# Turning the second layer's attention weights by VectorE squares and SBUF transfers, in place of TensorE

## The chip, the cores and the metric

The kernel runs on one core of a Trainium2 chip. The core has five engines that each run their own list of instructions in order and wait for one another by semaphores: TensorE (PE; its weight loads are shown as PEld), VectorE (DVE), ScalarE (ACT), GpSimd (POOL) and SyncE (SP), which here issues nearly all transfers. The metric is the device time of one execution in microseconds. Before the change it is 584.42 us, the median of three runs (584.39 to 584.82).

## The reference

One inference step of a two-layer decoder, for a prompt of 256 positions and 8 single sample positions, 264 columns in all, with model width 1024. The change touches the second layer's attention of the prompt, eight heads of width 64:

```python
def stick_breaking_attention(q, k, v, q_pos):
    # A[t,s] = sigmoid(z_ts) * prod_{s<j<t} (1 - sigmoid(z_tj)), strictly causal
    ...
        z = jnp.einsum('bqhd,bkhd->bhqk', qh, k).astype(jnp.float32) * scale
        before = kpos[None, :] < pos[:, None]
        log_keep = jnp.where(before, jax.nn.log_sigmoid(-z), 0.0)
        later = lax.cumsum(log_keep, axis=3, reverse=True) - log_keep
        w = jnp.where(before, jnp.exp(jax.nn.log_sigmoid(z) + later), 0.0)
        return jnp.einsum('bhqk,bkhd->bqhd', w.astype(v.dtype), v)
```

The rest of the step (the projections, the first layer, pooling, the feed-forward parts, the output norm) is not changed.

## The kernel before, in words

All weights are streamed from HBM in a fixed order, as blocks of 128×128. A tile of work is eight blocks; a transfer (`raw`) brings sixteen blocks, and three `raw` buffers take turns. ScalarE copies each tile to a high part (`wh`, L318), VectorE takes the rest as a low part (`wl`, L325), and TensorE does three matmuls of 264 columns per block (`mm`). The phases are the input projection, attention, output projection and feed-forward of each layer. The order on TensorE is written out: `run` goes through the blocks, and hooks put other work behind a block of a given number. In the second layer the order is kept as written for TensorE and for the transfers on SP (`late`); on VectorE and ScalarE a scheduler places the instructions when the program is built, and it then stays as it is.

The second layer's input projection gives u, q, k and v in this order, 32 blocks each, four tiles of 128 rows; a row tile is a pair of heads. An evicted tile of v is `v4b` (L1252). For the attention:

- `z_qk` (blocks 83 and 103) makes the scores Z of a pair in PSUM. For each head there are three squares of 128×128: queries 0 to 127 with keys 0 to 127, queries 128 to 255 with keys 0 to 127, queries 128 to 255 with keys 128 to 255. The second query block with its own keys is the third square.
- `stick` has ScalarE make sigmoids, VectorE a scan along the keys (`keep`, L1140) and a product (`w`, L1141). The product w has the queries on its partitions, 128 rows of 384 columns.
- `z_tr` turns the three squares of each head of a pair by TensorE (`pt`, three transposes of a head in one PSUM bank), and ScalarE copies a head's bank to SBUF (`pT`, L1171). The four pairs stand behind blocks 93, 102 and 122 of the input projection and block 2 of the output projection.
- `v_pair` transposes a tile of v4b (`vtp_v`), behind blocks 113, 123, 127 and block 3 of the output projection.
- `z_av` (block 8 of the output projection, right behind the sample's value matmuls `pv_l`) multiplies values with turned weights into `pav`, pair after pair.

There are four PSUM banks for `mm` and its kin and four (`at`) for Z, pt, pav and the like. Five buffers hold w, two hold keep. SP's list is one queue in order: an issue whose wait is not over holds up all issues behind it.

Of the kernel before, what the change touches and what calls it, by code (L numbers as in the profile page):

```python
# [13 lines left out]
AF = mybir.ActivationFunctionType  # L14
# [4 lines left out]
P = 128  # L19
D = 1024  # L20
KD = D // P
SEQ = 256
# [5 lines left out]
HD = 64  # L28
# [179 lines left out]
def tile_decoder_step(ctx: ExitStack, tc: tile.TileContext, a):  # L208
    nc = tc.nc
    v, s, g = nc.vector, nc.scalar, nc.gpsimd  # L210
# [14 lines left out]
    pe = TensorE()  # L225
# [13 lines left out]
    def f4(name, shape=(P, 4, T), dt=F32):  # L239
        return up.tile(list(shape), dt, tag="u", name=name)  # L240

    def mv(name):
        return [f4(f"{name}_{x}", (P, 4, TP), F32R)[:, :, X0:X0 + T] for x in "hl"]
# [4 lines left out]
    def at(name):  # L248
        return psa.tile([P, 512], F32, tag="at", name=name)
# [17 lines left out]
    def cst(n):  # L267
        o, w = _CST[n]
        return CST[:, o:o + w]
# [11 lines left out]
    def late(dst, src):  # L281
        tc.keep_in_program_order(nc.sync.dma_start(dst, src))
# [21 lines left out]
    turned = {}  # L304
# [86 lines left out]
    first, o = [], 0  # L391
# [29 lines left out]
    ident = cst("ident")  # L421
# [15 lines left out]
    class Norm:  # L437

        def __init__(self, name):
            self.name, self.acc = name, None  # L440
# [38 lines left out]
    def halves(h, l, src):  # L479
        s.activation(h, src, AF.Copy)  # L480
        v.tensor_tensor(l, src, h.bitcast(F32), ALU.subtract)  # L481
# [72 lines left out]
    def v_pair(vt, src, t, name, bank=None):  # L554
        p = (bank or at)(f"vtp_{name}{t}")
        for kb in range(2):
            pe.transpose(p[:, kb * P:(kb + 1) * P], src[:, kb * P:(kb + 1) * P], ident)
        s.activation(vt[:, :, t * P:(t + 1) * P], p[:, :2 * P].rearrange("p (b d) -> p b d", b=2), AF.Copy)

    def av(pav, vt, w, h):  # L560
        o = pav[64 * (h % 2):64 * (h % 2) + 64, :SEQ]
        pe.matmul(o, vt[:, 0, h * HD:(h + 1) * HD], w[:, :SEQ], start=True, stop=False)
        pe.matmul(o[:, P:], vt[:, 1, h * HD:(h + 1) * HD], w[:, SEQ:], start=False, stop=True)

    def gelu_set():
        tc.keep_in_program_order(s.preload_act_table_set("gelu_apprx_tanh_and_others"))
# [4 lines left out]
    def lnexp():  # L571
        tc.keep_in_program_order(s.preload_act_table_set("natural_log_exp_and_others"))
# [285 lines left out]
    vt = f4("vt0", (P, 2, 512))  # L858
# [36 lines left out]
    def s_av(t):  # L895
        if t == 0:
            catA.extend(mv("catA0"))
        w = st0.pop(("pT", t))
        pav = at(f"pav0_{t}")
        for hh in range(2):  # L900
            av(pav, vt, w[:, hh, :], 2 * t + hh)
        halves(catA[0][:, t, :SEQ], catA[1][:, t, :SEQ], pav[:, :SEQ])


# [124 lines left out]
    blk = lambda b, f, *x: hk.at(b / 8 - 1, f, *x)  # L1029
# [52 lines left out]
    for t in range(4):  # L1082
        blk(8, s_av, t)
# [24 lines left out]
    vt = f4("vt1", (P, 2, 512))  # L1108
# [6 lines left out]
    st1 = {}  # L1115
# [17 lines left out]
    def stick(w, z, t):  # L1133


        n, keep = 384, keeps[t % 2]
        for a0, a1 in ((1, P), (P + 1, n)):
            s.activation(keep[:, a0:a1], z[:, a0:a1], AF.Sigmoid, scale=-1.0)
        s.activation(w, z, AF.Sigmoid)
        v.tensor_tensor_scan(keep[:, 1:n][:, ::-1], keep[:, 1:n][:, ::-1], edge[:, 1:][:, ::-1], 0.0, ALU.mult, ALU.max)  # L1140
        v.tensor_tensor(w, w, keep[:, 1:], ALU.mult)  # L1141

    def stick_all(w, z):
# [5 lines left out]
        v.tensor_tensor_scan(keep[:, ::-1], keep[:, ::-1], edge[:, P:P + 1].to_broadcast([P, n]), 1.0, ALU.mult, ALU.max)  # L1149
        v.tensor_tensor(w[:, :n - 1], w[:, :n - 1], keep[:, 1:], ALU.mult)  # L1150

    def z_qk(t):
        pss = [at(f"Z1_{2 * t + i}") for i in range(2)]
        hd = [(q4[b:b + 64, t, :], k4[b:b + 64, t, :]) for b in (0, 64)]
        for ps, (qh, kh) in zip(pss, hd):
            pe.matmul(ps[:, 0:P], qh[:, 0:P], kh[:, 0:P], start=True, stop=False, skip_group_check=True)
        for ps, (qh, kh) in zip(pss, hd):
            pe.matmul(ps[:, P:384], qh[:, P:SEQ], kh[:, 0:SEQ], start=False, stop=True, skip_group_check=True)
        for i, ps in enumerate(pss):
            w = st1["w", 2 * t + i] = pp.tile([P, 384], F32, tag="p", name=f"w1_{2 * t + i}")  # L1160
            stick(w, ps[:, :384], 2 * t + i)
        if t == 3:
            lnexp()

    def z_tr(t):
        pT = st1["pT", t] = f4(f"pT1_{t}", (P, 2, 384))
        for hh in range(2):
            w, pt = st1.pop(("w", 2 * t + hh)), at(f"pt1_{2 * t + hh}")
            for i in range(3):
                pe.transpose(pt[:, i * P:(i + 1) * P], w[:, i * P:(i + 1) * P], ident)  # L1170
            s.activation(pT[:, hh, :], pt[:, :384], AF.Copy)  # L1171

    def z_av(t):
        if t == 0:
            catA.extend(mv("catA1"))
        pav, pT = at(f"pav1_{t}"), st1.pop(("pT", t))
        for hh in range(2):
            av(pav, vt, pT[:, hh, :], 2 * t + hh)
        halves(catA[0][:, t, :SEQ], catA[1][:, t, :SEQ], pav[:, :SEQ])

    def zs_score():
# [74 lines left out]
    blk = lambda b, f, *x: hk.at(b / 8 - 1, f, *x)  # L1256
# [5 lines left out]
    for t in range(4):  # L1262
        blk((83, 103)[t // 2], z_qk, t)
    blk(82, zs_tr)
    for t, b in enumerate((93, 102, 122, 130)):
        if b < 128:
            blk(b, z_tr, t)
    blk(84, late, a["poolp"], plp)
    blk(84, late, a["pools"], PALL)
    blk(112, late, a["k1"], k4)  # L1270
# [5 lines left out]
        blk(b, lambda t=t: v_pair(vt, v4[:, t, :], t, "v1", mmb))  # L1276
    run(orders["in1"], pick(xg), in1_evac, hk)
    hk = Hooks()
    for t, b in enumerate((93, 102, 122, 130)):
        if b >= 128:  # L1280
            blk(b - 128, z_tr, t)
    blk(3, lambda: v_pair(vt, v4[:, 3, :], 3, "v1"))
    for i in range(2):
        blk(8, sample_av_of(st1, PZ, vtiles, i, "l1"))
    for t in range(4):
        blk(8, z_av, t)
# [79 lines left out]
```

## Time and profile before

| | us |
|---|---|
| median of 3 runs | 584.42 |
| the profiled execution | 584.75 |
| its span | 583.0 |
| TensorE busy in the span | 578.1 |
| VectorE busy | 420.4 |
| ScalarE busy | 345.6 |
| second layer's attention, from Z to the last pav | 332.5 to 365.7 |

The span is the time between the first and last instruction that the profiler saw; 1.75 us lie around it. In the page's groups, a row names the line, the engine, the operation, output and inputs, the count, then busy time and the mean of one. The busy time of matmuls overlaps, since they are pipelined: a matmul of 264 columns is busy for some 0.28 us, and the next starts 0.12 us after it. In the chain, the lengths are what each piece adds to the end. In a timeline, a row gives the start, the length, the engine, the line, the operation, and in brackets the engine's idle time before it with what ended it. Line L220 is the helper of all matmuls, L223 that of all transposes on TensorE, L282 that of the transfers, so tiles tell the rows apart.

### The profile page before, as it was taken

The page shows a single profiled execution, that of the slowest core. Times are in us where ns is not written, and L with a number is a line of the kernel's source. Part 1 is how long each engine was busy: PE and PEld are TensorE (multiplying, and loading weights), DVE is VectorE, ACT ScalarE, POOL GpSimd, SP SyncE. Part 2 cuts the span into 40 slices and gives each one's busy share as a digit, 9 for nine tenths or more (in the row PEclk, how much of TensorE's full clock was granted, in tenths as well). Part 3 has the DMA queues.
Part 4 walks back from the last instruction along what each step waited for, and adds up shares of the span by engine and source line. Part 5 has one row for each costly group of instructions (what it writes and reads, how often), then busy time and mean ns, then how long its engine had stood idle before and what let it go on. Part 6 is the DMA issues. An engine that isn't in the chain of part 4 may idle for free.

```text
span 583.0 us, 12326 instructions
## 1 busy us (share of the span) xinstructions
PE 578.1 (99%) x4913; PEld 563.9 (97%) x4913; DVE 420.4 (72%) x742; ACT 345.6 (59%) x617; POOL 110.7 (19%) x107
## 2 busy tenths in 40 slices
PE   9999999999999999999999999999999999999997
PEld 8998979999999999999999897999999999999996
DVE  6999766877777777665659685587777777765441
ACT  7748955775555656654454576667646565565442
POOL 1110021222323232210120000132232222221010
PEclk9999999999999999999999999999999999999999
DMA  8997973555454545796567855254545455556501
GB/s 343 361 376 256 402 266 105 186 175 187 161 201 152 209 150 212 265 388 221 182 230 262 311 207 181 83 209 146 201 161 191 171 183 180 175 194 223 211 2 75
DMA packets 27707, 122.40 MB, mean 210 GB/s; under 512 B 3330, under 2 KB 4226, under 8 KB 16258
## 3 DMA queue, kind: packets, MB, share of 16 engines
q1 hardware_dynamic: 27648, 121.62, 58.1%
q8 instruction: 38, 0.62, 0.4%
q14 instruction: 19, 0.16, 0.1%
q10 hardware_dynamic: 2, 0.00, 0.0%
HBM read 117.65 MB, written 3.96 MB: 209 GB/s over the span
## 4 chain that ended last, share of the span: by engine, by line
PE 95%; issue 2%; DMA 1%; ACT 1%; DVE 0%; POOL 0%; POOLq 0%; ACTq 0%
PE mm L220 88%; DMA V<-in_vp 1%; PE pv_l L220 1%; PE sc L220 1%; PE pav L220 1%; PE pt L223 1%; PE warm L220 1%; PE Z L220 1%; PE S L220 1%; ACT wh L318 0%; PE pf L220 0%; DVE bv L995 0%; PE vtp_v L223 0%; PE pm L220 0%; ACT bu L1025 0%
## 5 line engine op out<-in xcount | busy, mean ns | idle before, releaser
L325 DVE TENSOR_TENSOR wl<-raw,wh 128x1024 fp32r<-128x1024 f32 x178 | 218.4, 1231 | 64.2 <-ACT wh L318 63.8
L318 ACT ACTIVATE wh<-raw 128x1024 fp32r<-128x1024 f32 x178 | 186.2, 1051 | 81.0 <-PE mm L220 70.0
L220 PE MATMUL mm<-xg_f_h,wh 128*128 128x264 f32 x704 | 197.8, 281 | 0.0
L220 PE MATMUL mm<-xg_f_h,wl 128*128 128x264 f32 x704 | 197.8, 281 | 0.0
L220 PE MATMUL mm<-xg_f_l,wh 128*128 128x264 f32 x704 | 197.5, 280 | 0.0
L220 PEld LDWEIGHTS mm<-xg_f_h,wh 128*128 128x128 f32 x704 | 131.9, 187 | 0.0
L220 PEld LDWEIGHTS mm<-xg_f_h,wl 128*128 128x128 f32 x704 | 131.9, 187 | 0.0
L220 PEld LDWEIGHTS mm<-xg_f_l,wh 128*128 128x128 f32 x704 | 131.9, 187 | 0.0
L623 POOL TENSOR_TENSOR wk<-wk 128x264 f32<-128x264 f32 x44 | 67.3, 1531 | 193.1 <-DVE wk L622 142.8
L220 PE MATMUL mm<-a_h,wl 128*128 128x264 f32 x330 | 92.7, 281 | 0.0
L220 PE MATMUL mm<-a_h,wh 128*128 128x264 f32 x330 | 92.7, 281 | 0.0
L220 PE MATMUL mm<-a_l,wh 128*128 128x264 f32 x330 | 92.6, 280 | 0.0
L480 ACT ACTIVATE a_h<-wk 128x264 fp32r<-128x264 f32 x44 | 18.6, 424 | 75.0 <-POOL wk L623 75.0
L220 PEld LDWEIGHTS mm<-a_l,wh 128*128 128x128 f32 x330 | 61.8, 187 | 0.0
L220 PEld LDWEIGHTS mm<-a_h,wl 128*128 128x128 f32 x330 | 61.8, 187 | 0.0
L220 PEld LDWEIGHTS mm<-a_h,wh 128*128 128x128 f32 x330 | 61.8, 187 | 0.0
L481 DVE TENSOR_TENSOR a_l<-wk,a_h 128x264 fp32r<-128x264 f32 x44 | 19.2, 437 | 43.2 <-ACT a_h L480 43.2
L220 PE MATMUL mm<-xg_h,wl 128*128 128x264 f32 x160 | 42.9, 290 | 0.0
L220 PE MATMUL mm<-xg_h,wh 128*128 128x264 f32 x160 | 42.7, 289 | 0.0
L220 PE MATMUL mm<-xg_l,wh 128*128 128x264 f32 x160 | 41.9, 283 | 0.0
L220 PE MATMUL mm<-xg_n_h,wl 128*128 128x264 f32 x128 | 36.9, 288 | 0.0
L220 PE MATMUL mm<-xg_n_h,wh 128*128 128x264 f32 x128 | 36.0, 281 | 0.0
(273 smaller groups left out, 934.0 us busy)
## 6 DMA issues: line engine op xcount, KB each, us to landing
raw<-in_w SPq DMA_DIRECT2D x89, 1024.0 KB, 4.8
K<-in_kt SPq DMA_DIRECT2D x32, 256.0 KB, 7.3
V<-in_vp SPq DMA_DIRECT2D x32, 256.0 KB, 6.2
raw<-in_w SPq DMA_DIRECT2D x3, 512.0 KB, 6.1
xw<-in_xw SPq DMA_DIRECT2D x3, 388.0 KB, 4.8
X<-in_x SPq DMA_DIRECT2D x4, 264.0 KB, 7.0
out_y<-y SPq DMA_DIRECT2D x3, 256.0 KB, 2.2
out_k<-k SPq DMA_DIRECT2D x1, 528.0 KB, 7.8
```

The source lines that it names most:

```text
L220: return self.keep(nc.tensor.matmul(*x, **k))
L223: return self.keep(nc.tensor.transpose(*x, **k))
L318: i = s.activation(h, src, AF.Copy)
L325: i = v.tensor_tensor(l, src, h.bitcast(F32), ALU.subtract)
L480: s.activation(h, src, AF.Copy)
L481: v.tensor_tensor(l, src, h.bitcast(F32), ALU.subtract)
L623: g.tensor_tensor(A, A, C, ALU.mult)
```

## The change

Of each head's three squares the first two, those with keys 0 to 127, are no longer turned by TensorE. When two pairs of heads are done, VectorE turns w's first 256 columns of each of these four heads in squares of 32×32 (`squares`, STREAM_TRANSPOSE), into the tile `turnN_squares`. There each square is turned, but it still lies in the 32 partitions that it came from. Transfers inside SBUF (`move`) then take the squares to the partitions of their keys, in the tile `turnN_turned`: for each of four partition groups of the source and each of four groups of the goal one transfer, which carries two times 128 columns on 32 partitions. That makes 16 transfer instructions for four heads and 32 for eight; each carries two blocks, 64 in all. They stand on SP behind the hooks of blocks 103 and 119.

The third square stays with TensorE: `z_own` turns those of four heads into one PSUM bank, behind block 102 and behind block 2 of the output projection, and one ScalarE copy of 512 columns brings them to SBUF. `av` reads the turned tile for keys 0 to 127 (columns in runs of 32) and that copy for the rest.

```diff
-    def av(pav, vt, w, h):
+    def av(pav, vt, w0, w1, h):
         o = pav[64 * (h % 2):64 * (h % 2) + 64, :SEQ]
-        pe.matmul(o, vt[:, 0, h * HD:(h + 1) * HD], w[:, :SEQ], start=True, stop=False)
-        pe.matmul(o[:, P:], vt[:, 1, h * HD:(h + 1) * HD], w[:, SEQ:], start=False, stop=True)
+        pe.matmul(o, vt[:, 0, h * HD:(h + 1) * HD], w0, start=True, stop=False)
+        pe.matmul(o[:, P:], vt[:, 1, h * HD:(h + 1) * HD], w1, start=False, stop=True)
+
+    class Turn:
+        def __init__(self, name):
+            self.name = name
+            self.src, self.dst = [f4(f"{name}_{x}", (P, 8, 4, 32)) for x in ("squares", "turned")]
+        def squares(self, i, w):
+            v.transpose(self.src[:, :, i, :], w[:, :SEQ].rearrange("p (c b) -> p c b", b=32))
+        def move(self, i):
+            for j in range(4):
+                late(self.dst[32 * j:32 * j + 32, i::4], self.src[32 * i:32 * i + 32, j::4])
+        def of(self, i):
+            return self.dst[:, :, i, :]
...
     def z_qk(t):
...
+        if t % 2:
+            turns.append(Turn(f"turn{t // 2}"))
+            for i in range(4):
+                turns[-1].squares(i, st1["w", 2 * t - 2 + i])
...
-    def z_tr(t):
-        pT = st1["pT", t] = f4(f"pT1_{t}", (P, 2, 384))
-        for hh in range(2):
-            w, pt = st1.pop(("w", 2 * t + hh)), at(f"pt1_{2 * t + hh}")
-            for i in range(3):
-                pe.transpose(pt[:, i * P:(i + 1) * P], w[:, i * P:(i + 1) * P], ident)
-            s.activation(pT[:, hh, :], pt[:, :384], AF.Copy)
+    def z_own(f):
+        pt = at(f"pt1_{f}")
+        for i in range(4):
+            pe.transpose(pt[:, i * P:(i + 1) * P], st1["w", 4 * f + i][:, SEQ:384], ident)
+        pT = st1["pT", f] = f4(f"pT1_{f}", (P, 4, P))
+        s.activation(pT, pt.rearrange("p (i q) -> p i q", q=P), AF.Copy)
...
-    for t, b in enumerate((93, 102, 122, 130)):
-        if b < 128:
-            blk(b, z_tr, t)
+    blk(102, z_own, 0)
+    for f, b in enumerate((103, 119)):
+        for i in range(4):
+            blk(b, lambda f=f, i=i: turns[f].move(i))
...
-    for t, b in enumerate((93, 102, 122, 130)):
-        if b >= 128:
-            blk(b - 128, z_tr, t)
+    blk(2, z_own, 1)
```

On VectorE the change adds eight instructions, and the scheduler places them between the others. At the end of the input projection, VectorE's list before has these rows (`w1_6` is the product of head 6, `mm856` and `mm864` are the second and third tile of v in PSUM):

```order
L1141 TENSOR_TENSOR w1_6_4743<-w1_6_4743,keep0_4105 128x384
L325 TENSOR_TENSOR wl110_4763<-raw58_4492,wh110_4762 128x8x128
L1140 SCALAR_TENSOR_TENSOR keep1_4106<-keep1_4106,edge_4103 128x383
L1252 TENSOR_TENSOR v4b_4095<-mm856_4766,R_n1_4177 128x264
L1141 TENSOR_TENSOR w1_7_4749<-w1_7_4749,keep1_4106 128x384
L325 TENSOR_TENSOR wl111_4794<-raw58_4492,wh111_4793 128x8x128
L1252 TENSOR_TENSOR v4b_4095<-mm864_4797,R_n1_4177 128x264
```

And now, at the same place:

```order
L572 STREAM_TRANSPOSE turn1_squares_4746<-w1_5_4722 128x8x32
L325 TENSOR_TENSOR wl110_4776<-raw58_4492,wh110_4775 128x8x128
L1157 TENSOR_TENSOR w1_6_4734<-w1_6_4734,keep0_4105 128x384
L1156 SCALAR_TENSOR_TENSOR keep1_4106<-keep1_4106,edge_4103 128x383
L1274 TENSOR_TENSOR v4b_4095<-mm856_4779,R_n1_4177 128x264
L572 STREAM_TRANSPOSE turn1_squares_4746<-w1_6_4734 128x8x32
L1157 TENSOR_TENSOR w1_7_4740<-w1_7_4740,keep1_4106 128x384
L325 TENSOR_TENSOR wl111_4807<-raw58_4492,wh111_4806 128x8x128
L572 STREAM_TRANSPOSE turn1_squares_4746<-w1_7_4740 128x8x32
L1274 TENSOR_TENSOR v4b_4095<-mm864_4810,R_n1_4177 128x264
```

The turns of heads 5, 6 and 7 stand ahead of the third tile of v, the last one right before it, and the split `wl110` has moved ahead of the product of head 6. In the same way a turn stands between scan and product of heads 1 and 2, and four turns stand ahead of head 4's scan.

On SP, the list before around the same place (`raw60` to `raw62` are weights, `out_k1` and `out_v1` outputs):

```order
L282 DMA V1_14_4673<-in_vp1 128x512
L282 DMA raw60_4760<-in_w 128x2048
L282 DMA out_k1<-k4b_4094 128x1056
L282 DMA raw61_4827<-in_w 128x2048
L282 DMA raw62_4977<-in_w 128x2048
L282 DMA out_v1<-v4b_4095 128x1056
```

And now:

```order
L282 DMA V1_14_4668<-in_vp1 128x512
L282 DMA turn0_turned_4604<-turn0_squares_4603 32x2x128 x16
L282 DMA raw60_4773<-in_w 128x2048
L282 DMA out_k1<-k4b_4094 128x1056
L282 DMA turn1_turned_4747<-turn1_squares_4746 32x2x128 x16
L282 DMA raw61_4856<-in_w 128x2048
L282 DMA raw62_4991<-in_w 128x2048
L282 DMA out_v1<-v4b_4095 128x1056
```

The two groups of 16 transfers stand ahead of the weight transfers raw60 and raw61, and all behind them in the queue waits until they are issued.

More of the change, by code (lines that the diff above doesn't have):

```diff
@@ L900, in s_av @@
         for hh in range(2):
-            av(pav, vt, w[:, hh, :], 2 * t + hh)
+            av(pav, vt, w[:, hh, :SEQ], w[:, hh, SEQ:], 2 * t + hh)
         halves(catA[0][:, t, :SEQ], catA[1][:, t, :SEQ], pav[:, :SEQ])
@@ L1150, in stick_all @@
         v.tensor_tensor(w[:, :n - 1], w[:, :n - 1], keep[:, 1:], ALU.mult)
+    turns = []
     def z_qk(t):
@@ L1175, in z_av @@
             catA.extend(mv("catA1"))
-        pav, pT = at(f"pav1_{t}"), st1.pop(("pT", t))
+        pav = at(f"pav1_{t}")
         for hh in range(2):
-            av(pav, vt, pT[:, hh, :], 2 * t + hh)
+            i = 2 * t % 4 + hh
+            av(pav, vt, turns[t // 2].of(i), st1["pT", t // 2][:, i, :], 2 * t + hh)
         halves(catA[0][:, t, :SEQ], catA[1][:, t, :SEQ], pav[:, :SEQ])
```

## The prediction

> **What bounds the kernel now.** I read first the page's busy shares and its chain of waits (the work that ended last, followed back from the end).
>
> ```profile
> span 583.0 us, 12326 instructions
> PE 578.1 (99%) x4913; PEld 563.9 (97%) x4913; DVE 420.4 (72%) x742; ACT 345.6 (59%) x617; POOL 110.7 (19%) x107
> PE 95%; issue 2%; DMA 1%; ACT 1%; DVE 0%; POOL 0%; POOLq 0%; ACTq 0%
> ```
>
> TensorE sets the time: 95% of the chain, with nothing between its matmuls in most stages. So what leaves TensorE is a gain, unless TensorE then waits for what does the work instead. The same chain in order of time shows what TensorE does at the places of the change (start, length, count):
>
> ```profile
> 337.85 0.66 PE pt L223 x6
> 342.48 0.66 PE pt L223 x6
> 352.25 0.66 PE pt L223 x6
> 356.23 0.66 PE pt L223 x6
> 362.85 2.80 PE pav L220 x32
> 367.29 0.44 PE po_l L223 x4
> ```
>
> The 24 transposes of the second layer's weights take 4 × 0.66 us and TensorE is on the chain at each. VectorE's 72% over the span says little here, so its timeline in this stretch comes next (start, length, engine, line; in brackets the idle time before a row):
>
> ```profile
> 336.60 0.56 DVE L1141 TENSOR_TENSOR w<-w,keep 128x384 f32<-128x384 f32 x1
> 340.92 0.55 DVE L1141 TENSOR_TENSOR w<-w,keep 128x384 f32<-128x384 f32 x1
> 343.27 0.48 DVE L1243 SCALAR_TENSOR_TENSOR catB_l<-pm,VEC,catB_h 128x264 fp32r<-128x264 f32 x1
> 344.97 0.95 DVE L1140 TENSOR_TENSOR_SCAN keep<-keep,edge 128x383 f32<-128x383 f32 x1 [1.22 <-ACT keep L1138]
> 346.03 0.56 DVE L1141 TENSOR_TENSOR w<-w,keep 128x384 f32<-128x384 f32 x1
> 346.50 0.95 DVE L1140 TENSOR_TENSOR_SCAN keep<-keep,edge 128x383 f32<-128x383 f32 x1
> 347.37 0.40 DVE L1252 TENSOR_TENSOR v4b<-mm,R_n 128x264 f32<-128x264 f32 x1
> 351.69 0.40 DVE L1252 TENSOR_TENSOR v4b<-mm,R_n 128x264 f32<-128x264 f32 x1
> 352.01 0.55 DVE L1141 TENSOR_TENSOR w<-w,keep 128x384 f32<-128x384 f32 x1
> 353.61 0.42 DVE L1252 TENSOR_TENSOR v4b<-mm,R_n 128x264 f32<-128x264 f32 x1
> 355.55 0.43 DVE L1252 TENSOR_TENSOR v4b<-mm,R_n 128x264 f32<-128x264 f32 x1 [0.38 <-PE mm L220]
> ```
>
> From 334 to 355 us VectorE has one pause, the 1.22 us ahead of the scan at 344.97. It is nearly full just where the change puts eight more instructions on it. The products w (L1141) and the evicted values v4b (L1252) are what TensorE reads next: v4b is transposed (vtp_v), in TensorE's fixed order.
>
> **The part on TensorE.** Of 24 transposes 8 stay, in two groups of four. The po_l row has the price of such a four, 0.44 us. Gain 4 × 0.66 − 2 × 0.44 = 1.76 us: 0.66 at 337.85, 0.22 at 342.48, 0.66 at 352.25, 0.22 at 356.23. The value matmuls keep number and size. They read the turned tile in runs of 32 columns; no row shows such a read, and I take it as free (bounds: 0, and the 2.80 us twice, if each read took double).
>
> **The part on VectorE.** A VectorE instruction frees the engine before its own end, so I count from start to start. No row shows a turn in squares; the nearest is the shuffle in the first layer:
>
> ```profile
> 29.10 0.46 DVE L845 STREAM_SHUFFLE rz_q<-mm 128x264 f32<-128x264 f32 x1
> 29.45 0.41 DVE L847 SCALAR_TENSOR_TENSOR q<-mm,rope 128x264 f32<-128x264 f32 x1
> ```
>
> It holds the engine for 0.35 us for 264 columns, and ends 0.46 us after its start. For 256 columns I take 0.35 us and 0.45 us. The upper bound is the scan, the row that costs most per column: 0.87 us (346.50 to 347.37) for 383, so 0.58 us for 256. The lower bound is the scaling of the plain eviction: w to the next row, 0.47 us for 384 columns (346.03 to 346.50), so 0.31 us.
>
> Now the new order. A w that stands directly behind its scan starts 1.06 us after it (344.97 to 346.03); anything else starts after 0.87. A turn between the two so costs 0.19 us less than its 0.35. Up to the row at 343.27 come four turns, and for two heads the gap is filled: 4 × 0.35 − 2 × 0.19 = 1.02, so it starts at 344.29. With three turns ahead of it, w of the fourth head moves from 340.92 to 340.92 + 1.05 − 0.38 = 341.59. The fifth scan follows the row at 344.29 by 0.40 us, at 344.69: 0.28 earlier than now, since the pause of 1.22 is eaten up and TensorE's Z comes earlier too. From there two more turns stand ahead of v4b of the second pair, with one gap filled: 351.69 − 0.28 + 0.70 − 0.19 = 351.92. For the third pair it is all four: 353.61 − 0.28 + 1.40 − 0.19 = 354.54. The fourth turn of this group ends right before, at 354.64 with its tail.
>
> **What TensorE then waits for.** The two rows that read v4b, and the weight load ahead of the second:
>
> ```profile
> 353.11 0.38 PE L223 MATMUL vtp_v<-CST,v4b 128*128 128x128 f32 x2
> 354.66 0.25 PEld L223 LDWEIGHTS vtp_v<-CST,v4b 128*128 128x128 f32 x2
> 354.76 0.38 PE L223 MATMUL vtp_v<-CST,v4b 128*128 128x128 f32 x2
> ```
>
> The transposed tile is the loaded one, so 0.10 us (354.66 to 354.76) follow its readiness. Three waits come of it:
> - The fourth own transpose at 342.32 (the chain's 342.48 less its offset of 0.16, as at vtp_v) − 0.66 + 0.33 = 341.99; its w is ready at 341.59 + 0.55 + 0.10 = 342.24. Wait 0.25.
> - vtp_v of the second pair would come at 353.11 − 1.54 + 0.25 = 351.82; v4b is ready at 351.92 + 0.40 + 0.10 = 352.42. Wait 0.60.
> - vtp_v of the third pair would come at 354.76 − 1.54 + 0.85 = 354.07; v4b is ready at 354.54 + 0.42 + 0.10 = 355.06. Wait 0.99.
>
> Behind each stand all of TensorE's further matmuls. The fourth pair (355.55, behind a pause) is not late: TensorE is then back on today's times. Sum: 0.25 + 0.60 + 0.99 − 1.76 = **+0.08 us**. By the bounds of a turn (eight lie ahead of the last wait) it is 8 × (−0.04) + 0.08 = −0.24 and 8 × 0.23 + 0.08 = +1.92.
>
> **The part on the queue and the transfers.** The order shows 32 transfer instructions, 16 for each group, of 32 KB and 64 runs of 512 bytes. They stand in SP's one queue, whose first of each group waits for the fourth turn, with the weight loads behind it. Rows on SP and of DMA issues:
>
> ```profile
> 41.59 0.42 SPq L282 DMA_DIRECT2D sguc<-in_sguw  x1
> 42.06 0.42 SPq L282 DMA_DIRECT2D sguc<-in_sgub  x1
> 343.37 0.34 SPq L282 DMA_DIRECT2D raw<-in_w  x1
> 353.72 4.50 SPq L282 DMA_DIRECT2D raw<-in_w  x2
> 327.39 0.65 SPq L282 DMA_DIRECT2D out_pools<-PALL  x1
> out_y<-y SPq DMA_DIRECT2D x3, 256.0 KB, 2.2
> raw<-in_w SPq DMA_DIRECT2D x89, 1024.0 KB, 4.8
> 372.13 1.06 ACT L318 ACTIVATE wh<-raw 128x1024 fp32r<-128x1024 f32 x1 [1.86 <-PE mm L220]
> ```
>
> Back to back an issue takes 0.47 us (41.59 to 42.06); alone 0.34; for out_pools 0.65, my upper bound. Landing is 2.2 us on an idle queue. No row shows a transfer inside SBUF; I take 0.43 (the busy 0.42 and a step) and 2.2. The first group starts near 343.3 and has landed before 353, nine microseconds ahead of pav. The second starts at 354.64: last issue 354.64 + 15 × 0.43 = 361.1, landed 363.3. TensorE needs it half-way through pav, 362.85 + 1.40 + 0.08 = 364.33. Hidden by 1.0 us, under sample matmuls and half of pav; with 0.47 by 0.4; with 0.65 not.
>
> The weight chunk issued at 343.37 goes out near 350.5, and the one of 353.72 near 361.6; landed 4.8 later, 366.4, while ScalarE splits it at 372.13 for want of TensorE. These loads stay hidden by over 5 us. ScalarE has 2 evictions for 8 and is not the bound. Its eviction of the first four has a Z bank to free, some 0.8 us ahead of its use.
>
> **The rivals.**
> - *All of the gain arrives*: VectorE's turns cost TensorE nothing. For it speaks the chain, which has no VectorE in this stretch; against it the full timeline. It gives −1.76 us. Chance 0.14.
> - *The second group of transfers is late* (the other side). The place is pav of the third pair; it decides from (364.33 − 2.2 − 354.64) / 15 = 0.50 us per issue. With 0.65 and 2.2 the last lands at 366.6: with the 0.08 that makes **+2.3 us**. For it: many small runs, the long issues of out_pools, output of k still in flight. Against it: 64 runs, half of those of the rows above. Chance 0.18. [...]
> - *A turn costs like a scan*, 0.58 us: **+1.9 us** by the bound above. Chance 0.10. [...] Against it speaks the shuffle's row.
> - *64 issues*, as the change's name says, instead of 32: this is the late-transfer rival at twice the issues; the order shows 32, so I leave it inside that chance.
>
> **How the numbers follow.** Forecast, chance 0.58: the gain and the three waits cancel, +0.1 us on the span of 583.0. The profiled execution took 584.75 and the median of the runs shown is 584.42; the same +0.1 gives **584.5 us**. Its own range is −0.7 to +1.0: the turn's bounds, and slips of a few tenths at each wait. The cases around it are 582.7, 586.8 and 586.3. The range of 8 in 10 is 583.3 to 586.4: it leaves out the full gain and the far end of late transfers. A change under 0.2% (1.17 us) can't be told from none. Faster by more: 0.14 and the edge of the forecast, 0.16. Slower by more: 0.10 for the turn, 0.14 of the late transfers, a little of the forecast: 0.26. The rest, 0.58, is the same.
>
> **What would show it.** Right: TensorE has 16 pt matmuls fewer, and waits of 0.2 to 1 us with VectorE as releaser ahead of the own transposes and ahead of two of the vtp_v rows; VectorE without the 1.22 us pause; pav without a DMA wait. Wrong: vtp_v in step with today's rows less 1.5 us (full gain), pav released by a turned transfer (late transfers), or turns that stand 0.5 us and more from the next row.

## The result and the profile after

The changed kernel takes 591.19 us (median of 4 runs, 590.4 to 591.7), the kernel before 584.4 (4 runs beside them). The ratio is 1.0114, with a 95% interval of 1.0097 to 1.0132: slower by 6.8 us. The profiled execution took 590.4 us with a span of 588.6, 5.6 longer than the span before; it is the fastest of the four, with a mean granted clock of 0.996, where the other three have 0.992 or 0.993. One execution in this document was in a slower state (631.74 us at a mean clock of 0.85, of the kernel with out_k moved), and nothing is read from it.

The page of the changed kernel: span, busy shares, and the chain's shares by engine.

```profile
span 588.6 us, 12339 instructions
PE 578.3 (98%) x4897; PEld 563.2 (96%) x4897; DVE 422.6 (72%) x750; ACT 344.1 (58%) x611; POOL 111.8 (19%) x107
PE 93%; DMA 2%; issue 2%; SPq 1%; DVE 1%; POOL 0%; ACT 0%; POOLq 0%; ACTq 0%
```

TensorE has lost the 16 matmuls (4913 to 4897), and its share of the chain has gone from 95% to 93%, with DMA and SP's queue in its place. The waits of TensorE between 300 and 400 us name the place (us in total, times, longest):

```profile
PE pav L220 <- DMA turn_turned<-turn_squares: 4.5, 1, 4.5
PE vtp_v L223 <- DVE v4b L1274: 1.1, 2, 0.8
```

The second row is what the prediction's main term spoke of. The first is the rival: the value matmuls of the third pair wait for the turned transfers. To size both, one landmark in front and one behind are needed, since the two executions stand 0.65 us apart already ahead of the changed stage, in the first layer. ns_n and ns_f are the norm's matmuls on both sides. The chain of the kernel before and, in the second fence, of the changed kernel (start, length, count):

```profile
302.82 0.24 PE ns_n L220 x2
392.17 0.25 PE ns_f L220 x2
```

```profile
302.17 0.24 PE ns_n L220 x2
353.59 7.50 DMA out_k<-k4b
361.11 0.59 SPq L282
366.22 1.83 DMA turn_turned<-turn_squares
368.14 2.71 PE pav L220 x16
397.80 0.25 PE ns_f L220 x2
```

Before, the stage is 392.17 − 302.82 = 89.35 us, now 95.63: the whole loss of this execution, 6.28 us, lies in it (5.6 on the span, since the 0.65 us of the first layer go the other way). TensorE's timeline around pav, before and then changed, shows it:

```profile
362.78 2.87 PE L220 MATMUL pav<-pT,vt 128*64 128x256 f32 x32
```

```profile
362.03 0.66 PE L220 MATMUL pav<-turn_turned,vt 128*64 128x256 f32 x4
363.16 0.44 PE L220 MATMUL pav<-pT,vt 128*64 128x128 f32 x4
368.14 1.01 PE L220 MATMUL pav<-turn_turned,vt 128*64 128x256 f32 x4 [4.54 <-DMA turn_turned<-turn_squares]
```

First, TensorE comes to pav at 362.03 − 302.17 = 59.86 us after ns_n. Before it was 362.78 (the timeline's start; the chain's row is 362.85) − 302.82 = 59.96. So the transposes and VectorE's waits nearly cancel: −0.10 us. Second, after four pav groups there is a wait of 4.54 us. Third, the same rows are then slower: 1.01 us for what took 0.66. The windows of the changed kernel say why (window, its length, PE busy with count; the column after it is the granted clock, then the DMA share and GB/s):

```profile
364.00:368.00 4.00, 0.00 (x0) 1.00 0.20 49
368.00:369.00 1.00, 0.86 (x6) 0.66 0.82 147
369.00:370.00 1.00, 1.00 (x10) 0.50 0.93 393
370.00:371.00 1.00, 1.00 (x8) 0.50 1.02 434
371.00:372.00 1.00, 1.00 (x6) 0.64 1.03 377
372.00:373.00 1.00, 1.00 (x11) 1.00 0.91 279
```

The clock is halved for some 3.4 us, from just after work starts again. What is missing to 1.00 adds up to 0.34 + 0.50 + 0.50 + 0.36 = 1.70 us. Sum: −0.10 + 4.54 + 1.70 = 6.14 of the 6.28.

Why are the transfers late? SP's queue in that stretch (start, length of the group, count), and the rows of the turned tile (ns min/median/max) and of its DMA issues (KB each, median us to landing):

```profile
342.54 10.38 SPq L282 DMA_DIRECT2D turn_turned<-turn_squares  x16
353.02 0.52 SPq L282 DMA_DIRECT2D raw<-in_w  x1
353.59 0.43 SPq L282 DMA_DIRECT2D out_k<-k4b  x1
354.13 12.68 SPq L282 DMA_DIRECT2D turn_turned<-turn_squares  x16
L282 SPq DMA_DIRECT2D turn_turned<-turn_squares x32: 585/595/760, 342.5 to 366.2; - x32
turn_turned<-turn_squares SPq DMA_DIRECT2D x32, 32.0 KB, 1.9
```

One issue takes 0.595 us, and sixteen take 10.38, so 0.65 from issue to issue, not 0.43. The second group takes 12.68: SP waits in the middle of it. The waits of SP's queue there:

```profile
SPq L282 <- DMA out_k<-k4b: 1.3, 1, 1.3
SPq L282 <- DMA raw<-in_w: 1.1, 1, 1.1
```

The chain shows the first of these: out_k is issued at 353.59, lands 7.50 us later, and only then does the transfer of 361.11 go out. It is the eighth transfer behind out_k, and the weight chunk of 353.02 holds the transfer before, the eighth behind the chunk, in the same way (354.13 + 6 × 0.65 = 358.0, and 1.1 later 359.1). The waits and the places are the trace's; why it is the eighth, no run shows.

### The profile page after: what moved, and what is told of

It is laid out like the page before. It is cut to its first block, busy times and chain, and to the rows that moved or that the text cites. A ratio compares the mean times of both kernels' runs of the same rounds, so it can differ in the third digit from the quotient of the medians.

```text
span 588.6 us, 12339 instructions
## 1 busy us (share of the span) xinstructions
PE 578.3 (98%) x4897; PEld 563.2 (96%) x4897; DVE 422.6 (72%) x750; ACT 344.1 (58%) x611; POOL 111.8 (19%) x107
## 4 chain that ended last, share of the span: by engine, by line
PE 93%; DMA 2%; issue 2%; SPq 1%; DVE 1%; POOL 0%; ACT 0%; POOLq 0%; ACTq 0%
PE mm L220 87%; SPq L282 1%; DMA out_k<-k4b 1%; PE sc L220 1%; PE pav L220 1%; PE pv_l L220 1%; DMA turn_turned<-turn_squares 1%; PE warm L220 1%; PE pt L223 1%; PE S L220 1%; PE Z L220 0%; DVE wl L325 0%; PE pf L220 0%; PE pm L220 0%; DVE w L1157 0%
```

## The experiments

The theory from here on: what is lost is lost by the second group's late transfers, and the rest of the change is worth nothing either way. Most runs change one thing; where one changes more, it is said. "After" below means the changed kernel. The kernel before took 584.06 us (median of 19 runs) beside the runs without the transfers, with the same transfers read later, with out_k behind and with one run per partition; 584.29 (27 runs) beside the probe, the two queues, the run without the waits on VectorE and its control; 584.19 (15 runs) beside the repeat of out_k behind and the turns out of VectorE's full stretch; and 583.75 (one run) beside the last. In the edits shown, three dots stand for lines left out.

**Without the transfers.** The prompt's attention of the second layer is not computed rightly here: the value matmuls read the squares where they are.

```diff
-            return self.dst[:, :, i, :]
+            return self.src[:, :, i, :]
...
-    for f, b in enumerate((103, 119)):
-        for i in range(4):
-            blk(b, lambda f=f, i=i: turns[f].move(i))
```

> The change with its 32 transfers left out: the value matmuls read the squares where VectorE left them, so rows are out of place and the prompt's attention of the second layer is not computed; all else stays. Theory A (the transfers alone carry the loss: 0.64 us from issue to issue in SP's one queue, the second group landed 4.5 us late, then a low clock): 584.0 to 584.8, no wait at pav, three short waits of TensorE on VectorE of 1.1 to 1.8 us in sum, against 1.76 us less of transposes. Rival B (VectorE's turns or TensorE's reading in runs of 32 columns cost something too): 586 or more.

Measured: 584.11 us, ratio 1.0002 (0.9992 to 1.0011). In the chain pav is one piece again:

```profile
361.50 2.80 PE pav L220 x32
```

Its 2.80 us are those of before, though the tile of squares, laid out like the turned one, is read in runs of 32 columns: such a read costs nothing here. The waits on v4b stay at 1.1 us. So transposes, turns and VectorE's waits together are worth nothing that can be measured; the 6.8 us are the transfers'.

**The same transfers, read later.** The value matmuls of the last two pairs stand at block 21 of the next stage instead of 8.

```diff
-        blk(8, z_av, t)
+        blk((8, 21)[t // 2], z_av, t)
```

> The change with the value matmuls of the third and fourth pair of heads moved from block 8 to block 21 of the output projection, 4.7 us later on TensorE; transfers as in the change. Theory A (the loss is one wait at pav and the low clock behind it): the transfers land as late as before, but TensorE has other work until then, no wait, no low clock: 584.0 to 585.2. Rival C (the transfers slow the weight stream or other work too): 586 or more.

Measured: 584.36 us, ratio 1.0008 (0.9998 to 1.0017). The transfers go out as before (last issue 366.1), no wait is left at pav, the clock is 1.00 throughout. The stage from ns_n to ns_f is 89.63 us, 0.28 over before; doing pav in two pieces takes 2 × 1.50 us in the chain in place of 2.80, which is most of it. So the transfers cost nothing by their traffic that these runs resolve, only by their lateness.

**The output of k behind the second group.**

```diff
-    blk(112, late, a["k1"], k4)
+    blk(120, late, a["k1"], k4)
```

> The change with the output of k (528 KB) issued behind the second group in place of ahead of it. Theory A1 (out_k only delays the group: 0.5 us for its own issue, and 1.3 to 2 us since a later transfer of the group must wait until out_k has landed): the group starts at 353.7, 16 issues at 0.64 us, last landed at 365.2, TensorE waits 1.7 us in place of 4.5: 587.5 to 589. Rival A2 (the group is bound by its own issues and landings alone): 590.5 to 591.

Measured: 586.52 us, ratio 1.0045 (1.0028 to 1.0062). Three of the four executions took 586.38 to 586.52 at a mean granted clock of 0.999, the fourth 587.87 at 0.996. The kernel was run once more for its profile:

> The changed kernel with the output of k behind the second group of transfers, once more, for its profile (the timed runs gave 586.5 us, 2.5 over the kernel before). Question: what are the 2.5 us? Theory: one wait at pav of 2.0 to 2.6 us and full clock behind it, the stage from ns_n to ns_f 91.3 to 92.0 us. Rival: a shorter wait (about 1.2 us) and behind it 1 us or more of time at half clock, as in the changed kernel.

Measured: 587.95 us in this one execution, at a mean granted clock of 0.996. SP's queue, the waits of TensorE, and the windows behind the wait:

```profile
342.53 10.37 SPq L282 DMA_DIRECT2D turn_turned<-turn_squares  x16
353.00 0.52 SPq L282 DMA_DIRECT2D raw<-in_w  x1
353.80 10.52 SPq L282 DMA_DIRECT2D turn_turned<-turn_squares  x16
```

```profile
PE pav L220 <- DMA turn_turned<-turn_squares: 2.1, 1, 2.1
```

```profile
364.00:366.00 2.00, 0.30 (x3) 0.97 0.44 155
366.00:367.00 1.00, 1.00 (x10) 0.50 1.01 296
367.00:368.00 1.00, 1.00 (x10) 0.50 1.05 352
368.00:369.00 1.00, 1.00 (x7) 0.50 1.02 319
369.00:370.00 1.00, 1.00 (x9) 0.85 0.93 377
```

With out_k gone from ahead the second group takes 10.52 us like the first, and the wait falls from 4.54 to 2.08: out_k cost 2.46 us. Without it the group starts 0.33 us sooner and takes 2.16 less, since neither out_k nor the weight chunk then holds SP up. In this execution the half clock stays, though the wait is half as long. My expectation of 2.0 to 2.6 us for the wait came in, the full clock behind it did not: the stage is 93.18 us, 3.83 over before, of which 2.08 is wait and 1.7 clock. It is not the usual case: the three timed executions of 586.4 to 586.5 are 1.4 to 1.6 us shorter at a clock of 0.999, so by their times and clocks they had the wait without the halved clock; no trace of them was kept. What may decide it is taken up with the last run below.

**One run per partition.** The layout is turned around, so that each transfer moves one run of 1 KB per partition instead of two of 512 bytes.

```diff
...
-            v.transpose(self.src[:, :, i, :], w[:, :SEQ].rearrange("p (c b) -> p c b", b=32))
+            v.transpose(self.src[:, :, :, i, :], w[:, :SEQ].rearrange("p (n c b) -> p c n b", n=2, b=32))
...
-                late(self.dst[32 * j:32 * j + 32, i::4], self.src[32 * i:32 * i + 32, j::4])
+                late(self.dst[32 * j:32 * j + 32, i], self.src[32 * i:32 * i + 32, j])
...
```

> The change with squares and turned tile laid out so that each transfer has one run of 1 KB per partition in place of two runs of 512 bytes; number and size of the transfers stay, TensorE reads the tile with three strides. Theory A3 (an issue costs 0.6 us because of the shape with two runs): issues of 0.34 to 0.47 us as for the weights, the second group landed by 362.5, no wait at pav: 584.0 to 585. Rival A4 (an issue costs 0.6 us whatever the runs, because both ends lie in SBUF or only 32 partitions take part): 0.6 us again, 590.5 to 591.5.

Measured: 591.57 us, ratio 1.013 (1.0113 to 1.0147).

```profile
L282 SPq DMA_DIRECT2D turn_turned<-turn_squares x32: 507/589/724, 342.3 to 365.7; - x32
```

The issue takes 0.589 us with half the runs. The number of runs is not what it is paid for. This trace also shows that the half clock can last longer than in the changed kernel:

```profile
364.00:368.00 4.00, 0.41 (x2) 0.80 0.31 66
368.00:372.00 4.00, 4.00 (x23) 0.50 0.91 346
372.00:376.00 4.00, 4.00 (x31) 0.85 0.83 293
```

What is missing to 1.00 is 4 × (0.20 + 0.50 + 0.15) = 3.4 us, so 6.8 us at half clock, of which the first 1.2 are still the wait at pav (4.25 us here). The mean clock of this execution is 0.994 and that of its three companions 0.993, near the 0.992 and 0.993 of the changed kernel's three executions without a trace. Those were 0.6 to 1.3 us longer than the profiled one, so they probably lost more by the clock than its 1.70 us.

**What one issue costs.** The kernel before, with four groups of four extra transfers at a time when SP's queue is idle, whose results nobody reads: inside SBUF with 32 and with 128 partitions, from HBM to 32 partitions, from 32 partitions to HBM.

```diff
...
+    for n, b in enumerate((26, 33, 40, 47)):
+        for i in range(4):
+            p32, p32b = slice(32 * i, 32 * i + 32), slice(32 * (i ^ 1), 32 * (i ^ 1) + 32)
+            d, x = ((dst[0][p32b, i], src[p32]), (dst[1][:, i], src), (dst[2][p32b, i], a["edge"][p32, :256]), (scratch[p32b], src[p32]))[n]
+            blk(b, late, d, x)
```

> The kernel before, with four groups of four transfers on SP's queue far behind the changed place, at a time when the queue is idle. What is asked is the busy time of one issue. Group 1: inside SBUF, 32 partitions, 32 KB, runs of 1 KB (like the transfers of the change in one run). Group 2: inside SBUF, 128 partitions, 128 KB. Group 3: from HBM to 32 partitions, 32 KB. Group 4: from 32 partitions to HBM, 32 KB. Theory A4 (the price of an issue comes of both ends lying in SBUF): groups 1 and 2 at 0.55 to 0.62 us, groups 3 and 4 at 0.33 to 0.47. Rival (it comes of an end on only 32 partitions): groups 1, 3 and 4 at 0.55 to 0.62, group 2 at 0.33 to 0.47. Rival (it comes of a source in SBUF, as with out_pools at 0.65): groups 1, 2 and 4 at 0.55 to 0.65, group 3 at 0.33 to 0.47. Rival (it came of the busy queue alone): all below 0.47. The time is that of the kernel before, 584 us, within 0.3.

Measured (ns min/median/max of an issue; first the two groups inside SBUF in this order, then from HBM, then to HBM):

```profile
L282 SPq DMA_DIRECT2D prdst<-edge x4: 571/592/642, 371.1 to 373.1; - x4
L282 SPq DMA_DIRECT2D prdst<-edge x4: 465/570/600, 373.7 to 375.9; - x4
L282 SPq DMA_DIRECT2D prdst<-in_edge x4: 420/420/531, 376.5 to 378.0; - x4
L282 SPq DMA_DIRECT2D scratch<-edge x4: 419/420/428, 378.9 to 380.3; - x4
```

The theory of both ends in SBUF holds in this one execution (583.9 us): 0.592 us with 32 partitions and 0.570 with 128, against 0.420 with one end in HBM. An issue inside SBUF cost 0.17 and 0.15 us more at the two sizes tried; the 128-partition transfer has four times the bytes for nearly the same price. Why it costs more is open. The long rows of the kernel before, out_pools at 0.65 among them, are not explained by this.

**Two queues.** The transfers with odd j go by SP's queue as before, those with even j by GpSimd's.

```diff
-                late(self.dst[32 * j:32 * j + 32, i::4], self.src[32 * i:32 * i + 32, j::4])
+                tc.keep_in_program_order((nc.sync if j % 2 else nc.gpsimd).dma_start(self.dst[32 * j:32 * j + 32, i::4], self.src[32 * i:32 * i + 32, j::4]))
```

> The changed kernel, with half of the transfers (eight of each group) issued by GpSimd's queue and half by SP's. Theory A (the transfers are late because one queue issues sixteen of them at 0.64 us each): eight issues take 5.1 us, SP's half of the second group has landed by 361.5, and if GpSimd issues at no more than 1.1 us each its half has landed by 365; the wait at pav of 4.5 us goes, with it the half clock behind it, and the time is 584.2 us (583.8 to 585.0). Rival 1 (GpSimd issues at 1.3 us or more): last issue of its half after 366, the wait stays at 2 us or more, 587 to 591. Rival 2 (what is slow is not the issue, but the transfers share something behind the queues): each queue then issues at about twice 0.64, and the last landing stays at 367 to 368, time 591.

Measured: 584.87 us, ratio 1.001 (1.0 to 1.0019).

```profile
L576 SPq DMA_DIRECT2D turn_turned<-turn_squares x16: 594/596/1091, 342.4 to 358.7; - x16
L576 POOL DMA_DIRECT2D turn_turned<-turn_squares x16: 536/536/705, 343.0 to 358.0; - x16
```

GpSimd issues in 0.536 us. The last issue is at 358.7 instead of 366.2, pav does not wait, the stage is 89.28 us. The first group now holds SP for only 5.26 us, so out_k goes out at 348.35 and holds nothing up. So the lateness was the serial issuing in one queue, with what it pushed. SP's queue keeps its pace while GpSimd's works (0.596 us against 0.595); GpSimd's was not measured alone.

The time is still 0.6 us over the kernel before, though the stage is not longer. Part of it lies outside the span: 2.1 to 2.2 us in all ten executions, against 1.7 to 1.8 in the 27 of the kernel before. The run with late turns below, the only other one that issues on GpSimd's queue, has the same 2.1 to 2.2, and no other execution has over 1.9. Why is not shown.

**Without the waits on VectorE.** After, with the value matmuls late, out_k behind the second group, and the transposes of the values (vtp_v) moved away from VectorE's full stretch:

```diff
...
-    for t, b in enumerate((113, 123, 127)):
+    for t, b in enumerate((113, 126)):
...
-    blk(3, lambda: v_pair(vt, v4[:, 3, :], 3, "v1"))
+    blk(3, lambda: v_pair(vt, v4[:, 2, :], 2, "v1"))
+    blk(5, lambda: v_pair(vt, v4[:, 3, :], 3, "v1"))
...
```

> The changed kernel with what the earlier runs point to: the value matmuls of the last two pairs later (block 21 of the next stage instead of 8), the output of k behind the second group of transfers, and the transposes of the new values of the second pair at block 126 instead of 123, of the third at block 3 of the next stage and of the fourth at block 5, so that TensorE does not meet v4b before VectorE has made it. Theory: the 1.76 us of transposes saved are a gain once no wait takes them back; the waits on VectorE of 0.28 and 0.81 go, only the 0.2 ahead of the own transposes is left, so 584.1 - 1.5 = 582.5 us (582.2 to 583.2). Rival 1 (the places of the transposes of the values only shift the waits to other rows): 583.7 to 584.4. Rival 2 (other matmuls fill TensorE less well, the clock or the weight loads cost it): above 584.4.

> Control for the mended kernel: the kernel before with only the new places of the transposes of the values (second pair at block 126, third at block 3, fourth at block 5 of the next stage). Theory: the kernel before has no wait on VectorE there, so nothing is gained: 584.0 us, within 0.3. Rival: these places are worth something by themselves, 583.5 or less, and then that much of the mended kernel's gain is not that of the change.

Measured: 584.3 us (11 runs), ratio 1.0 (0.9991 to 1.0009), where 582.5 was expected. The control, the kernel before with these places alone, 584.46, ratio 1.0003 (0.9994 to 1.0012): the places by themselves are worth nothing. In the mended kernel's timeline the 1.1 us of waits at vtp_v have gone, and another has come:

```profile
354.11 0.39 PE L220 MATMUL mm<-catB_h,wl 128*128 128x264 f32 x1 [0.51 <-DVE v4b L1274]
361.38 0.66 PE L220 MATMUL pav<-turn_turned,vt 128*64 128x256 f32 x4
```

Now an ordinary mm waits for VectorE's v4b to free its accumulator, and pav comes 0.6 us earlier than in the changed kernel, not 1.1. The first rival of that run was right as to the direction: where the transposes stand only moves part of the wait to the next thing that needs VectorE. The stage is 89.00 us, 0.35 under before, less than the runs resolve.

**The turns out of VectorE's full stretch.** The mended kernel, in which the second group's turns stand behind all four v4b, and both groups use two queues; out_k is where the changed kernel has it. So against the mended kernel three things differ at once.

```diff
...
-            for i in range(4):
+            for i in range(4 if t == 1 else 0):
                 turns[-1].squares(i, st1["w", 2 * t - 2 + i])
...
+    for i in range(4):
+        blk(6, lambda i=i: turns[1].squares(i, st1["w", 4 + i]))
+    for i in range(4):
+        blk(6, lambda i=i: turns[1].move(i))
...
```

> The mended kernel, in which TensorE still waited 0.5 us for v4b, with the four turns of the second group taken out of VectorE's full stretch (they stand behind all four v4b, in block 6 of the next stage) and both groups of transfers on two queues, SP's and GpSimd's. Theory (VectorE's full stretch is what gives the saved transposes back, wherever the waits then show): the 0.51 us of wait on v4b go and TensorE comes to pav about 1.5 us earlier than in the kernel before (today 60.0 us after ns_n, then 58.3 to 58.7); the value matmuls in two pieces cost 0.28 us; no wait at pav for transfers. Time 582.8 us (582.4 to 583.4) where the kernel before has 584.1 to 584.3. Rival 1 (TensorE is given back its waits elsewhere, by the bank that v4b frees or by ScalarE's splits): pav at 59.2 us or more after ns_n, time 583.6 or more. Rival 2 (the later transfers are late again): a wait at pav of 0.5 us or more, time 584 or more.

Measured: 583.53 us (11 runs), ratio 0.9989 (0.998 to 0.9998). The four late turns run on VectorE from 355.15 us. TensorE's first pav and the two landmarks:

```profile
360.14 0.66 PE L220 MATMUL pav<-turn_turned,vt 128*64 128x256 f32 x4
```

```profile
301.81 0.24 PE ns_n L220 x2
389.93 0.25 PE ns_f L220 x2
```

TensorE's matmuls have no wait left between 300 and 400 us, and it comes to pav 360.14 − 301.81 = 58.33 us after ns_n, 1.63 earlier than before: nearly all of the 1.76. Where the transfers and out_k go does not bear on this, as TensorE meets neither ahead of pav. The stage is 88.12 us, 1.23 less than before. The timed gain, 0.66 us (0.1 to 1.2), is just short of the 582.4 to 583.4 expected. The span alone is 1.0 us shorter (medians of 581.4 and 582.4); the rest goes into the 2.1 to 2.2 us outside it, as with two queues above. It is the only version that beats the kernel before, and by little.

**How long a wait halves the clock.** The kernel with out_k behind, and the last two pairs' value matmuls two blocks later.

```diff
...
-        blk(8, z_av, t)
+        blk((8, 10)[t // 2], z_av, t)
```

> The kernel with the output of k behind the second group of transfers (there TensorE waited 2.08 us at pav and then ran for 3.4 us at half clock), with the value matmuls of the last two pairs two blocks later (block 10 of the stage instead of 8, about 0.8 us of matmuls between). The wait becomes about 1.2 us (1.0 to 1.5). Theory H1 (any wait that empties TensorE for more than about 1 us is followed by the half clock): the granted clock is 0.50 for 3 us or more behind it, the stage from ns_n to ns_f is 92.4 us or more. Rival H2 (it needs about 2 us without work): full clock behind the wait, stage 90.5 to 91.3 us. In the kernel before it is 89.35.

Measured: 585.74 us in this one execution, stage 90.99 us.

```profile
PE pav L220 <- DMA turn_turned<-turn_squares: 1.3, 1, 1.3
```

```profile
365.00:366.00 1.00, 0.21 (x2) 1.00 0.62 231
366.00:367.00 1.00, 1.00 (x14) 1.00 1.14 350
```

Here a wait of 1.27 us leaves the clock at 1.00; one of 2.08 us halved it in the profiled execution above. That is as the second theory has it, with one execution on each side. The transfers keep the DMA engines as busy here (share 1.14) as behind the halved waits, so their traffic alone is not what lowers the clock.

But the length of the wait alone may not decide: the three executions with out_k behind kept a clock of 0.999. The clock records of the traces show when it changes. In the changed kernel it falls after 361.813 us at full, is full again 3.413 us later, and stays so for 215.040 us, nearly to the end; in the kernel before it stays full for 576.852 us. These are 106, 1, 63 and 169 times 3.4133 us. With out_k behind and with one run per partition the clock is halved for 3.4 and 6.8 us by the windows shown. In the 3.413 us that end at the fall, TensorE had no matmul for 3.24 us in the changed kernel, for 2.08 with out_k behind, and for some 3.05 with one run per partition. The 1.30 us without a matmul in the 3.413 us before these in the changed kernel, and the 1.27 us here, left the clock full. So a wait of 2 us that is cut in two by the border between two such stretches might pass, which would explain those three executions; this is a guess, and without their traces it is not shown.

## Why the prediction was wrong

It forecast 584.5 us and no change; 591.19 was measured, outside its range. The step that failed is the price of one issue inside SBUF, and with it the 1.0 us of cover for the second group; two terms behind it, out_k and the clock, stood at nothing. Point by point:

- *TensorE's gain and the waits on VectorE.* Right in place and in sum. The turns take 0.34 us from start to start (0.35 assumed), VectorE's pause of 1.22 us is eaten up, and the waits stand where they were forecast. The trace gives 0.28 and 0.81 us of idle time ahead of the vtp_v rows of the second and third pair. Counted from start to start, as in the forecast, TensorE is held 0.44 and 0.96 us there (a matmul still counts as busy for 0.16 us when the next could start), and 0.17 ahead of the own transposes; 0.60, 0.99 and 0.25 were forecast. At pav the balance is −0.10 us against the +0.08 forecast, and without the transfers the time is that of before (584.11 us against 584.06).
- *Reading the turned tile.* Right: free (2.80 us for pav without the transfers, as before).
- *One issue of a transfer inside SBUF.* Here it failed. I took 0.43 us "(the busy 0.42 and a step)" from rows of transfers out of HBM, less than the 0.47 from issue to issue that the same rows gave; it is 0.65, which was the upper bound I had named, and past the 0.50 from which the second rival decides. I had held against that rival that there are only half as many runs, and the run with one run per partition shows that runs are not what is paid for. By the prediction's own sum the last transfer then lands at 354.64 + 15 × 0.65 + 1.9 = 366.3 instead of 363.3, 2.0 us behind the 364.33 at which TensorE needs it. The wait with out_k out of the way is 2.08. So the rival's mechanism, its place and the price of this piece were right, though its 586.8 us has only this piece of the loss, and the 1.0 us of cover that made it the less likely case was a price taken from the wrong kind of row. No row of before had both ends in SBUF, and there the nearest rows were not near enough to choose the middle.
- *The queue.* Not foreseen: the first group's issues take 10.4 us and push out_k from 343.76 to 353.59, right ahead of the second group, where its own landing (7.50 us) holds a transfer of the group up, after the weight chunk has held up the one before. This cost 2.46 us. I had named out_k as speaking for the rival and had given it no price, though it was behind a queue that I had just filled.
- *What stands behind a long wait.* Not foreseen: the halved clock, 1.70 us in the profiled execution.
- *The weight loads behind the queue.* Right: TensorE has no wait for them, though the second goes out at 366.91 and not near 361.6.

The three pieces, 2.08 + 2.46 + 1.70 = 6.24, are the loss of the profiled execution; the first alone gives about 586.5, as in three of the four executions with out_k behind.

The other half of the question is why the gain did not arrive even with the transfers away. The runs show it: VectorE is full between 334 and 355 us (20.79 of 21.00 busy in the changed kernel), so what its turns displace comes back to TensorE as a wait, at vtp_v or, when that is moved, at the bank of the next mm. Only in the run with the turns taken out of that stretch does TensorE keep 1.63 of its 1.76 us.

## What to carry to other kernels

Price a transfer by its issue on the queue first (sixteen of 32 KB held SP's for 10.4 us here, where the median one landed in 1.9), then by bytes, and take the price from a row with the same two ends (0.59 us in the probe, against 0.42 with one end in HBM); where there is none, a sum that turns on it is open, not hidden. When a change puts many issues on a queue, list what these push later (here out_k, by 9.83 us) and ask what the pushed transfers then hold up. Before work is taken from the engine that bounds, look whether the one that gets it is full in the same stretch: here this gained nothing (with the waits at vtp_v and pav moved away, 584.3 us against 584.29 before) until half of it was put elsewhere in time, which gained 0.66 us.

## What the runs showed of the hardware

- An issue with both ends in SBUF took 0.57 to 0.60 us (medians) on SP's queue, with 32 or 128 partitions, one or two runs per partition, and 0.42 with one end in HBM in the same probe. On GpSimd's queue it took 0.536, and SP's kept its 0.596 beside it. The two runs with GpSimd's queue had some 0.36 us more outside the span.
- A transfer of 7.50 us that stands in a queue ahead of small ones held one of them up for 1.3 us, with the whole queue behind it.
- TensorE's clock was halved for 3.4 us after waits of 4.54 and 2.08 us, at a loss of 1.7 us each, and for 6.8 us from within one of 4.25; not after one of 1.27, and by the mean clock not in three of four executions whose wait should be near 2.08. Full rate was back 3.6 us after work began in the first two and 5.6 us in the third. In the traces of the two kernels the clock kept one value for 361.813, 3.413, 215.040 and 576.852 us, whole multiples of 3.4133. In one execution 2.08 us without a matmul were enough for the half clock.
